# Second product of the MLP: block products and plain chunks of a tile in shared PSUM banks, plain parts between block parts, and the tail's loads and low parts in another order

## Chip, cores and metric

One of the eight cores of a Trainium2 chip runs the kernel. The metric is the device time of one execution in microseconds (us). The kernel before takes 654.17 us (median of 3 runs, 653.78 to 654.19). One further execution was profiled; all trace rows come from it.

## The reference

One transformer block on 512 tokens of width 1024: RMSNorm, a mixed attention, an output projection, and then the part that matters here:

```
h = rmsnorm(x, mlp_pre_g)
a, u = split(h @ w_gate_up, [2816])
a = causal_dwconv(a, conv_w, conv_b)
y = (gelu(a) * u) @ w_down            # 2816 -> 1024: the second product
x = x + rmsnorm(y, mlp_post_g)
e = p @ w_ple
x = x + e * sigmoid(x @ w_ple_gate)   # the gate product
```

Everything is float32. The kernel splits each operand of a product into a high part and a low part and makes three TensorE products (high x high, low x high, high x low).

## The kernel before, in words

Tiles are 128 rows (features) by 512 columns (tokens). `w_down` has 22 chunks of 128 inner features and 8 output tiles of 128 rows. Output tiles 0 and 1 are computed plainly in `mlp_down`. The other six are computed in `down_pairs` (L1620) as three pairs, c = 0, 1, 2, each with two tiles i = 0, 1.

**Plain chunks.** Ten of the 22 chunks are multiplied as usual: `rest(c, i, k)` (L1700) takes five of them for tile i, k = 0 or 1, 15 matmuls of 512 columns into a PSUM bank of the tile (tag "mm"). For the last pair, `last(h, i)` (L1820) does it by token halves h, 30 matmuls of 256 columns for a half tile, into banks of its own.

**Block products.** The other twelve chunks go in three groups g through a 2x2 block scheme with seven products in place of eight (two output tiles x two inner chunks x two token halves). `token` (L1635) makes the sums of the token side, `sums` (L1671) those of the weights, `products` (L1683) issues 42 matmuls of 256 columns per group: 18 with the weights as loaded (part 0) and 24 with their sums (part 1). They end in four banks per pair; `blocks` (L1709) adds those up, `aside` (L1728) copies the plain result out of its bank, `finish` (L1733) adds the two, `square` (L1737) adds the squares to the running sum `acc` for the norm.

**Order.** `down_pairs` writes its order by hand: every step is put at a time with `at(t, f)`, the list is sorted by time and issued, and each step is kept in program order on its engine. So the times are only an order per engine: ScalarE (ACT) makes the high parts (`high`, L1661) and squares, VectorE (DVE) the low parts (`low`, L1665), sums and adds, GpSimd (POOL) the additions to `acc` and some low parts, SyncE (SP) issues every load. A step waits for its operands and for a free slot of its tile's tag ("wr" 2 slots, "wh" 6, "p" 6, "u" 26); what stands behind it on the same engine waits too. TensorE (PE) runs: plain chunks of pair 0, block parts of 0, plain chunks of 1, block parts of 1, block parts of 2, plain chunks of 2.

**The tail.** While the last pair runs, SP loads the attention's result x1 (`fetch` 0 to 3), four tiles of `w_ple_gate` (`gate(n, 0)`, L1810), two more of them for the next stage (issued by `weight` in `ple_gate`, L248) and the tiles of e (`fetch` 4 to 7, "r_away"). `gate(n, 1)` and `gate(n, 2)` make their high and low parts; three of the four low parts are on POOL (L1815). `out` (L1834) finishes a half tile: DVE adds (L1837), ACT squares (L1839), DVE adds to `acc` (L1841). When token half 0 of all tiles is in `acc`, `rstd_col` (L282, four small matmuls, then DVE and POOL) and `rstd_row` (L295) make the norm's factor "r4a"; then `norm_half` (L1263) applies it tile by tile on DVE and ACT, and `gate_half` (L1608) multiplies the four gate tiles with the result, first for half 0, then for half 1. `ple_gate` does the other four gate tiles and the output.

Of the kernel before, what the change touches and what calls it, by code (L numbers as in the profile page):

```python
# [15 lines left out]
P = 128  # L16
T = 512
# [26 lines left out]

TTAG = ["p"] * 4 + ["kn", "tt", "pt"] + ["u"] * 5
# [134 lines left out]
class Block:  # L180
# [1439 lines left out]
    def down_pairs(self, acc, yo, first):  # L1620
# [61 lines left out]
        def products(c, g, part):  # L1682
            z = w[c, g]  # L1683
            if g == 0 and part == 0:
                st[c]["z"] = [self.ps(t) for t in (["t", "t", "mm", "mm"] if c == 2 else "ssso")]
            key = ("raw", "sum")[part]
            todo = (((0, 0, 2, 0), (1, 2, 0, 0), (2, 7, 1, 0)), ((1, 6, 2, 1), (2, 5, 3, 0), (0, 4, 1, 1), (3, 3, 0, 1)))[part]
            for i, b, bank, half in todo:
                o = st[c]["z"][bank][:, HALF[half]]
                for k in range(2):  # L1690
                    x = yt[2 * g + k][b]
                    m = slice(i * W + k * P, i * W + k * P + P)
                    keep(mm(o, z[key, 0][:, m], x[:, 0, :], start=g + k + half == 0, stop=False, skip_group_check=True))
                    mm(o, z[key, 1][:, m], x[:, 0, :], start=False, stop=False, skip_group_check=True)
                    mm(o, z[key, 0][:, m], x[:, 1, :], start=False, stop=g == 2 and k == 1, skip_group_check=True)

        def rest(c, i, k):
            z = st[c]
            if k == 0:
                z["x", i] = self.ps("mm")  # L1700
            self.ordered = True
            wt = w[c, "x", i, k]
            for n in range(5):
                self.mm3(z["x", i], (wt["raw", 0], wt["raw", 1]), n * P, plain[5 * k + n], k + n == 0, k + n == 5)
            self.ordered = False

        def blocks(c, n):
            z = st[c]["z"]
            if n == 0:  # L1709
                if c == 2:  # L1710
                    yo.append(self.u([P, 2, T]))
                st[c]["q"] = self.s([P, T])
                if c < 2:
                    st[c]["r"] = self.s([P, T])
# [3 lines left out]
            m, q, s = yo[c + 1], st[c]["q"], st[c]["s"]  # L1718
            if n == 1:
                keep(add(s, s, z[2][:, H:]))  # L1720
                keep(add(q[:, H:], s, z[1][:, H:]))
            if n == 2:
                keep(add(s, s, z[3][:, :H]))
                keep(add(m[:, 0, :], q, z[0]) if c == 2 else add(q, q, z[0]))
            if n == 3:
                keep(add(halves(m[:, 1, :] if c == 2 else st[c]["r"]), s[:, None, :].broadcast_to([P, 2, H]), halves(z[1])))

        def aside(c, i):  # L1728
            if i == 0:
                yo.append(self.u([P, 2, T]))  # L1730
            keep(act.activation(yo[c + 1][:, i, :], st[c]["x", i], AF.Copy))

        def finish(c, i):  # L1733
            m = yo[c + 1][:, i, :]
            keep(add(m, m, st[c]["r" if i else "q"]))

        def square(c, i):  # L1737
            m = yo[c + 1][:, i, :]
            sq = self.s([P, T])
            keep(act.activation(sq, m, AF.Square))  # L1740
            keep(nc.gpsimd.tensor_add(acc, acc, sq))
# [14 lines left out]
        for u in xs(0) + gs(0) + xs(1) + gs(1) + gs(2) + xs(2):  # L1756
# [49 lines left out]
        def gate(n, k):  # L1806
# [152 lines left out]
```

## Time and profile before

| | |
|---|---|
| median of 3 runs | 654.17 us |
| the profiled execution | 655.45 us |
| its span (first to last instruction) | 653.7 us |
| PE busy in the span | 637.4 us (98%) |
| DVE busy | 530.6 us (81%) |
| ACT busy | 384.2 us (59%) |
| POOL busy | 153.5 us (23%) |

Times in rows count from the start of the span. A row of the timeline gives start, duration, engine, line, operation, output<-inputs, shapes, count, and in brackets how long the engine had been idle and whom it waited for. Matmuls overlap: their distance from start to start, not the duration shown, is what PE needs for one. The second product of the MLP in pairs runs from about 506 to 602 us, the norm and the four gate tiles to 626.7, the rest to 653.7.

### The profile page before, as it was taken

To read this page: it belongs to the slowest core of one execution; us is meant where nothing else is said; L and a number is where in the kernel's file an instruction comes from. 1 tells how busy PE (TensorE), PEld (TensorE's weight loads), DVE (VectorE), ACT (ScalarE), POOL (GpSimd) and SP (SyncE) were. 2 spreads that over 40 slices of the span, in tenths; PEclk is the share of its full clock that TensorE was granted. 3 is DMA by queue.
4 is the path that set the end of the run, shared out by engine and by line. 5 is a ranking of instruction groups with operands and counts; after the bars stand their busy time and mean duration, and the time that the engine had idled before them with its cause. 6 is when DMAs were issued, how large, how long until landed. Compare 5 with 4: busy or idle time off the path is not lost.

```text
span 653.7 us, 10857 instructions
## 1 busy us (share of the span) xinstructions
PE 637.4 (98%) x3865; PEld 567.7 (87%) x3865; DVE 530.6 (81%) x1118; ACT 384.2 (59%) x745; POOL 153.5 (23%) x225
## 2 busy tenths in 40 slices
PE   8999999999999999999998999999999999997996
PEld 8988887888787888888888999999988888996985
DVE  7794878988897559588999999999769775885972
ACT  7554689879999456265555565655656544342351
POOL 1112598668484310032020000000000001033000
PEclk9999999999999999999999999999999999997999
DMA  8437622210236466222413332432131323583031
GB/s 300 164 106 218 193 71 72 58 50 26 74 109 216 142 220 231 65 64 98 157 39 127 129 122 73 130 97 98 57 90 60 117 81 109 163 312 141 2 130 65
DMA packets 27719, 78.05 MB, mean 119 GB/s; under 512 B 3473, under 2 KB 4753, under 8 KB 27665
## 3 DMA queue, kind: packets, MB, share of 16 engines
q1 hardware_dynamic: 27520, 77.28, 36.0%
q8 instruction: 30, 0.49, 0.3%
q14 instruction: 25, 0.20, 0.1%
q10 hardware_dynamic: 144, 0.08, 0.1%
HBM read 63.72 MB, written 6.29 MB: 107 GB/s over the span
## 4 chain that ended last, share of the span: by engine, by line
PE 70%; DVE 15%; ACT 7%; issue 4%; DMA 3%; POOL 1%; ACTq 0%; SPq 0%; DVEq 0%
PE strassen_pss L1436 3%; PE strassen_pss L1439 3%; PE strassen_pss L1440 3%; PE nsa_pst L803 2%; PE nsa_pso L818 2%; PE r_pss L1184 2%; PE r_psmm L1184 2%; PE strassen_pst L1440 2%; PE strassen_pst L1439 2%; PE strassen_pst L1436 2%; PE mlpdown_psmm L255 1%; PE mlpdown_psmm L258 1%; PE mlpdown_psmm L259 1%; PE strassen_psmm L1439 1%; PE strassen_psmm L1436 1%
## 5 line engine op out<-in xcount | busy, mean ns | idle before, releaser
L590 POOL TENSOR_SCALAR nsa_u<-nsa_u,nsa_nrc,gate 128x512 f32<-128x512 f32 (+3 forms) x64 | 38.5, 612 | 21.6 <-DVE nsa_nrc L710 10.2
L1436 PE MATMUL strassen_pss<-sums_u,strassen_u 128*128 128x256 f32 x144 | 40.5, 282 | 1.7 <-ACT strassen_s L1447 1.7
L1749 POOL TENSOR_TENSOR mlpdown_s<-mlpdown_s,mlpdown_s 128x512 f32<-128x512 f32 x1 | 1.3, 1291 | 171.8 <-ACT mlpdown_s L1747 171.8
L1439 PE MATMUL strassen_pss<-sums_u,strassen_u 128*128 128x256 f32 x144 | 40.5, 281 | 0.0
L1440 PE MATMUL strassen_pss<-sums_u,strassen_u 128*128 128x256 f32 x144 | 40.5, 281 | 0.0
L602 ACT ACTIVATE nsa_u<-nsa_u,nsa_nnm 128x512 f32<-128x512 f32 (+3 forms) x64 | 35.3, 553 | 3.6 <-DVE nsa_nnm L598 3.3
L811 DVE TENSOR_TENSOR nsa_u<-nsa_pst,nsa_u 128x512 fp32r<-128x512 f32 x40 | 27.0, 688 | 9.8 <-ACT nsa_u L807 9.6
L1398 DVE TENSOR_TENSOR strassen_u<-strassen_u,strassen_u 128x1024 fp32r<-128x1024 f32 x27 | 33.3, 1237 | 0.0
L1661 ACT ACTIVATE mlpdown_u<-mlpdown_u 128x1024 fp32r<-128x1024 f32 (+1 forms) x15 | 15.0, 1013 | 28.0 <-DVE mlpdown_u L1680 18.7
L1394 ACT ACTIVATE strassen_u<-strassen_u 128x1024 fp32r<-128x1024 f32 x27 | 28.4, 1052 | 1.2 <-DVE strassen_u L1410 1.1
L1436 PEld LDWEIGHTS strassen_pss<-sums_u,strassen_u 128*128 128x128 f32 x144 | 27.2, 189 | 1.9 <-ACT strassen_s L1447 1.9
L818 PE MATMUL nsa_pso<-nsa_u,vnatural_u 128*128 128x512 f32 x80 | 28.0, 422 | 0.0
L1439 PEld LDWEIGHTS strassen_pss<-sums_u,strassen_u 128*128 128x128 f32 x144 | 27.2, 189 | 0.1
L1440 PEld LDWEIGHTS strassen_pss<-sums_u,strassen_u 128*128 128x128 f32 x144 | 27.2, 189 | 0.0
L807 ACT ACTIVATE nsa_u<-nsa_pst 128x512 fp32r<-128x512 f32 x40 | 23.3, 594 | 4.7 <-PE nsa_pst L803 4.1
L1330 POOL TENSOR_TENSOR mlpup_s<-mlpup_s,r3b 128x512 f32<-128x512 f32 x7 | 14.0, 2004 | 47.8 <-ACT mlpup_s L1302 42.8
L598 DVE CUSTOM_DVE_ANT_0 nsa_u<-nsa_pss,biastables_u 128x320 f32<-128x320 f32 (+3 forms) x64 | 24.7, 413 | 0.6 <-PE nsa_pss L595 0.5
L1665 DVE TENSOR_TENSOR mlpdown_u<-mlpdown_wr,mlpdown_u 128x640 fp32r<-128x640 f32 (+1 forms) x19 | 18.1, 951 | 8.8 <-ACT mlpdown_u L1661 8.8
L803 PEld LDWEIGHTS nsa_pst<-ident,nsa_u 128*128 128x128 f32 x160 | 18.9, 140 | 6.9 <-DVE nsa_u L811 1.3
L1440 PE MATMUL strassen_pst<-sums_u,strassen_u 128*128 128x256 f32 x88 | 24.8, 281 | 0.0
L1439 PE MATMUL strassen_pst<-sums_u,strassen_u 128*128 128x256 f32 x88 | 24.8, 281 | 0.0
L1436 PE MATMUL strassen_pst<-sums_u,strassen_u 128*128 128x256 f32 x88 | 24.7, 281 | 0.0
(637 smaller groups left out, 2504.5 us busy)
## 6 DMA issues: line engine op xcount, KB each, us to landing
strassen_wr<-in_gu_dram SPq DMA_DIRECT2D x14, 512.0 KB, 4.6
strassen_u<-in_gu_dram SPq DMA_DIRECT2D x14, 512.0 KB, 3.8
mlpup_wr<-in_gu_dram SPq DMA_DIRECT2D x10, 512.0 KB, 3.3
mlpdown_wr<-in_dn_dram SPq DMA_DIRECT2D x9, 512.0 KB, 3.5
mlpdown_wr<-in_dnx_dram SPq DMA_DIRECT2D x10, 320.0 KB, 3.0
projq_wr<-in_win_dram SPq DMA_DIRECT2D x5, 512.0 KB, 3.5
loadx_u<-in_xT_dram SPq DMA_DIRECT2D x8, 256.0 KB, 4.9
compress_u<-projk_u SPq DMA_DIRECT2D x16, 128.0 KB, 2.3
```

What stands on the lines that cost most here:

```text
L590: self.tc.keep_in_program_order(self.nc.gpsimd.tensor_scalar(ap, ap, col, gate, op0=ALU.mult, op1=ALU.mult))
L598: self.tc.keep_in_program_order(self.nc.vector.tensor_tensor_reduce(dst, src, bias, op0=ALU.add, op1=ALU.min, scale=slope, scalar=first, a ...
L602: self.tc.keep_in_program_order(self.nc.scalar.activation(p, p, AF.Exp, bias=nm, scale=-1.0, accum_out=sm))
L803: keep(nc.tensor.transpose(pt[:, r * P : (r + 1) * P], src, self.ident))
L811: keep(nc.vector.tensor_sub(t[:, 1, :], u["pt", j], t[:, 0, :].bitcast(F32)))
L818: keep(nc.tensor.matmul(u["po"], v, u["t", j][:, part, :], start=start, stop=u["left"] == 0))
L1184: keep(mm(ps, z["w", f"up{i}"][k][:, c * P : c * P + P], x, start=c + part + k == 0, stop=c == KC - 1 and part == 1))
L1394: keep(act.activation(hi, src, AF.Copy))
L1398: keep(sub(lo, src, hi.bitcast(F32)))
L1436: r = mm(ps, hi[:, o], x[:, 0, :], start=fresh and p == 0, stop=False, skip_group_check=not fresh)
L1439: mm(ps, lo[:, o], x[:, 0, :], start=False, stop=False, skip_group_check=not fresh)
L1440: mm(ps, hi[:, o], x[:, 1, :], start=False, stop=p == Q - 1, skip_group_check=not fresh)
```

## The change

1. **Shared banks.** The block products that only one tile needs go into the bank in which that tile's plain chunks are accumulated ("C" for tile 0, "D" for tile 1); two more banks ("U", "V") hold the products that both tiles need. Each pair has four banks, with its own tags. For half 1 of the last pair the tiles have further banks ("C1", "D1"). `aside` and `finish` go; `blocks` is one ACT copy and four adds of 256 columns; `join` adds SBUF and PSUM in one step. PE's matmuls are the same ones.
2. **Order on PE.** The two plain parts of tile 1 of pair 1 move between the block parts of pairs 1 and 2. In the tail, `rstd_col` and `rstd_row` stand one and two chunks of 3 matmuls later.
3. **Squares.** The addition to `acc` (`total`) is a step of its own, on POOL for pair 0 and on DVE for pair 1.
4. **Token sums.** The subtractions for the last token tile (5) come 6.6 us earlier in the list (9.6 for 16.2); the rest of it keeps its place.
5. **Loads and low parts of the tail.** x1 is fetched ahead of the gate tiles, the four gate tiles come next, then the two tiles for the next stage (now in the list, on SP behind gate tile 3), then e. All four gate low parts are on DVE. Some tags change.

```diff
+BANK = [dict(C="mm", D="mm", U="t", V="t"), dict(C="s", D="o", U="s", V="s"), dict(U="mm", V="mm", C="t", D="t", C1="s", D1="o")]
...
+        def product(c, g, n):
             z = w[c, g]
+            key, i, b, name, half = (("raw", 0, 0, "U", 0), ("raw", 1, 2, "C", 0), ("raw", 2, 7, "D", 0), ("sum", 1, 6, "U", 1), ("sum", 2, 5, "V", 0),
+                                     ("sum", 0, 4, "V", 1), ("sum", 3, 3, "C", 1))[n]
+            if c == 2 and n == 6:
+                name, half = "C1", 0
...
         def blocks(c, n):
...
-                keep(act.activation(st[c]["s"], z[2][:, :H], AF.Copy))
-                keep(act.activation(st[c]["q"][:, :H], z[2][:, :H], AF.Copy))
...
+                keep(act.activation(st[c]["q"][:, :H], z["U"][:, :H], AF.Copy))
+            q, r, u = st[c]["q"], st[c]["r"], st[c]["s"]
             if n == 1:
+                keep(add(u, q[:, :H], z["U"][:, H:]))
+                keep(add(q[:, H:], u, z["V"][:, H:]))
             if n == 2:
+                keep(add(r[:, :H], u, z["V"][:, :H]))
+                keep(add(r[:, H:], r[:, :H], z["V"][:, H:]))
-        def aside(c, i):
...
-        def finish(c, i):
...
+        def join(c, i):
             if i == 0:
                 yo.append(self.u([P, 2, T]))
+            keep(add(yo[c + 1][:, i, :], st[c]["qr"[i]], st[c]["z"]["CD"[i]][0]))
         def square(c, i):
...
+        def total(c, i):
+            keep((vec if c else nc.gpsimd).tensor_add(acc, acc, st[c]["sq", i]))
...
-        for u in xs(0) + gs(0) + xs(1) + gs(1) + gs(2) + xs(2):
+        for u in xs(0) + gs(0) + xs(1)[:2] + gs(1) + xs(1)[2:] + gs(2) + xs(2):
...
-                at((-12.0, -9.0, -6.0, -3.0, 2.6, 16.2)[t] + 0.8 * n, lambda t=t, n=n: token(t, n))
+                at((-12.0, -9.0, -6.0, -3.0, 2.6, 16.2 if n else 9.6)[t] + 0.8 * n, lambda t=t, n=n: token(t, n))
...
-                high(u, tags=(("kn", "tt"), ("u", "u"), ("u", "u"), ("wh", "wh"))[n])
+                high(u, tags=(("kn", "tt"), ("pt", "pt"), ("u", "u"), ("tt", "u"))[n])
             if k == 2:
-                low(u, eng=nc.gpsimd if n else vec)
+                low(u)
...
+        for n in range(2):
+            at(z + 26.0 + 0.01 * n, lambda n=n: next_gate(n))
         for n in range(4):
-            at(z + (5.3, 6.8, 13.0, 14.4)[n], lambda n=n: fetch(n))
-            at(z + 22.0 + 1.5 * n, lambda n=n: fetch(4 + n))
+            at(z + 5.3 + n, lambda n=n: fetch(n))
+            at(z + 26.1 + 0.01 * n, lambda n=n: fetch(4 + n))
             for k in range(3):
-                at(z + (11.8 + (0, 4.2, 6.2)[k], 13.4 + (0, 4.4, 5.4)[k], 15.4 + (0, 4.9, 5.9)[k], 17.0 + (0, 9.2, 10.6)[k])[n], lambda n=n, k=k: gate(n, k))
+                at(z + (10.8 + (0, 6.0, 6.8)[k], 11.8 + (0, 7.0, 7.6)[k], 15.4 + (0, 4.8, 5.4)[k], 16.8 + (0, 5.0, 7.8)[k])[n], lambda n=n, k=k: gate(n, k))
...
-        at(x + 2 * h, lambda: last(1, 0, range(5)))
-        at(x + 2.5 * h, lambda: w4.update(c=self.rstd_col(acc[:, HALF[0]], "r4a")))
-        at(x + 2.5 * h + 0.1, lambda: last(1, 0, range(5, 10)))
-        at(x + 3 * h, lambda: w4.update(r=self.rstd_row(w4["c"], "r4a", copy=False)))
+        at(x + 2 * h, lambda: last(1, 0, 0))
+        at(x + 2 * h, lambda: last(1, 0, 1, range(1)))
+        at(x + 2 * h + 2.2, lambda: w4.update(c=self.rstd_col(acc[:, HALF[0]], "r4a")))
+        at(x + 2 * h + 2.3, lambda: last(1, 0, 1, range(1, 5)))
         at(x + 3 * h + 0.1, lambda: out(1, 0, 0))
-        at(x + 3 * h + 0.2, lambda: last(1, 1))
+        at(x + 3 * h, lambda: last(1, 1, 0, range(2)))
+        at(x + 3 * h + 0.72, lambda: w4.update(r=self.rstd_row(w4["c"], "r4a", copy=False)))
+        at(x + 3 * h + 0.73, lambda: last(1, 1, 0, range(2, 5)))
+        at(x + 3 * h + 0.74, lambda: last(1, 1, 1))
```

## Rows read from the trace of the kernel before

**Rows 1.** The page: busy us of each engine, share of the span, instructions.
```profile
PE 637.4 (98%) x3865; PEld 567.7 (87%) x3865; DVE 530.6 (81%) x1118; ACT 384.2 (59%) x745; POOL 153.5 (23%) x225
```

**Rows 2.** Waits of PE over the span: waiting line, whom it waited for, us in total, times, longest us (those of the second product and of the norm behind it).
```profile
PE mlpdown_pst L282 <- DVE mlpdown_s L1841: 4.0, 1, 4.0
PE mlpdown_pss L1694 <- DVE mlpdown_u L1665: 0.7, 1, 0.7
PE norm_pss L259 <- DVE norm_u L1280: 0.6, 1, 0.6
PE mlpdown_psmm L1694 <- DVE mlpdown_u L1665: 0.2, 1, 0.2
```

**Rows 3.** Timeline of PE: the first plain matmul of the tail, the matmuls on both sides of the wait, and the first one after the four gate tiles.
```profile
580.25 0.28 PE L255 MATMUL mlpdown_pss<-mlpup_u,mlpdown_u 128*128 128x256 f32 x1
...
588.97 0.28 PE L258 MATMUL mlpdown_pss<-mlpup_u,mlpdown_u 128*128 128x256 f32 x1
589.09 0.28 PE L259 MATMUL mlpdown_pss<-mlpup_u,mlpdown_u 128*128 128x256 f32 x1
593.41 0.98 PE L282 MATMUL mlpdown_pst<-ones,mlpdown_s 128*128 128x1 f32 x4 [4.04 <-DVE mlpdown_s L1841]
...
597.17 0.41 PE L258 MATMUL mlpdown_pss<-mlpup_u,mlpdown_u 128*128 128x256 f32 x1
597.39 0.41 PE L259 MATMUL mlpdown_pss<-mlpup_u,mlpdown_u 128*128 128x256 f32 x1
...
602.15 0.28 PE L258 MATMUL norm_pss<-norm_u,mlpdown_u 128*128 128x256 f32 x1
603.02 0.39 PE L259 MATMUL norm_pss<-norm_u,mlpdown_u 128*128 128x256 f32 x1 [0.59 <-DVE norm_u L1280]
...
626.68 0.40 PE L255 MATMUL plegate_pst<-norm_u,plegate_wh 128*128 128x512 f32 x1
```

**Rows 4.** Busy time in a stretch of 1 us behind the wait: stretch, its length, then PE, PEld, DVE, ACT and POOL busy (and instructions), PE's granted clock, DMA share, GB/s.
```profile
595.00:596.00 1.00, 1.00 (x7) 1.00 (x6) 0.00 (x0) 0.00 (x0) 0.38 (x1) 0.50 0.06 25
```

**Rows 5.** The chain of work that ended last, in order of time: start, us, what.
```profile
580.45 9.04 DMA mlpdown_u<-in_wpg_dram
...
590.90 2.37 DVE mlpdown_s L1841
```

**Rows 6.** Timeline of ACT in the tail: high parts of gate tiles 0 and 1, of gate tile 2, and the square of the second half tile.
```profile
581.82 2.00 ACT L1661 ACTIVATE mlpdown_u<-mlpdown_u 128x1024 fp32r<-128x1024 f32 x2
...
589.51 1.06 ACT L1661 ACTIVATE mlpdown_u<-mlpdown_u 128x1024 fp32r<-128x1024 f32 x1 [1.33 <-DMA mlpdown_u<-in_wpg_dram]
590.47 0.40 ACT L1839 ACTIVATE mlpdown_s<-mlpdown_u 128x256 f32<-128x256 f32 x1
```

**Rows 7.** Timeline of DVE in the tail: three low parts of the last pair's plain weights, the first add of `blocks`, the low part of gate tile 0, the addition of the second half tile's squares to `acc`, and the second tile's addition in the norm.
```profile
580.17 1.46 DVE L1665 TENSOR_TENSOR mlpdown_u<-mlpdown_wr,mlpdown_u 128x640 fp32r<-128x640 f32 x1 [0.65 <-ACT mlpdown_u L1661]
581.55 1.55 DVE L1665 TENSOR_TENSOR mlpdown_u<-mlpdown_u,mlpdown_u 128x640 fp32r<-128x640 f32 x2
583.02 0.41 DVE L1720 TENSOR_TENSOR mlpdown_s<-mlpdown_s,mlpdown_psmm 128x256 f32<-128x256 f32 x1
...
585.52 1.87 DVE L1665 TENSOR_TENSOR mlpdown_u<-mlpdown_u,mlpdown_u 128x1024 fp32r<-128x1024 f32 x1
...
590.90 2.36 DVE L1841 TENSOR_TENSOR mlpdown_s<-mlpdown_s,mlpdown_s 128x256 f32<-128x256 f32 x1 [1.87 <-ACT mlpdown_s L1839]
...
600.51 2.12 DVE L1275 TENSOR_TENSOR mlpdown_u<-mlpdown_u,mlpdown_u 128x256 f32<-128x256 f32 x1
```

**Rows 8.** Timeline of POOL in the tail: low parts of gate tiles 2 and 3.
```profile
590.64 2.34 POOL L1665 TENSOR_TENSOR mlpdown_u<-mlpdown_u,mlpdown_u 128x1024 fp32r<-128x1024 f32 x1 [4.33 <-ACT mlpdown_u L1661]
...
599.80 2.55 POOL L1665 TENSOR_TENSOR mlpdown_u<-mlpdown_u,mlpdown_u 128x1024 fp32r<-128x1024 f32 x1 [4.42 <-ACT mlpdown_u L1661]
```

**Rows 9.** Timeline of SP: issues of gate tile 1, of a tile for the next stage, of gate tile 3, and of the first two of e; then, for the four gate tiles, the time from issue to landing; then, from the page, the loads of the block weights: count, KB of one, median us to landing.
```profile
576.08 0.38 SPq L1810 DMA_DIRECT2D mlpdown_u<-in_wpg_dram  x1
579.54 0.33 SPq L248 DMA_DIRECT2D plegate_wr<-in_wpg_dram  x1
...
582.04 0.92 SPq L1810 DMA_DIRECT2D mlpdown_u<-in_wpg_dram  x1
583.01 1.53 SPq L1803 DMA_DIRECT2D mlpdown_u<-r_away  x2
...
DMA to landing us min/median/max: 4.4/7.7/10.0
...
mlpdown_wr<-in_dn_dram SPq DMA_DIRECT2D x9, 512.0 KB, 3.5
```

**Rows 10.** Busy time in stretches of 2 us: columns as in rows 4.
```profile
578.00:580.00 2.00, 2.00 (x19) 2.00 (x18) 1.51 (x2) 1.13 (x2) 0.58 (x2) 1.00 1.05 346
...
590.00:592.00 2.00, 0.00 (x0) 0.00 (x0) 1.10 (x1) 0.87 (x2) 1.36 (x1) 1.00 1.04 424
```

**Rows 11.** Timeline of DVE and PE in the block parts of pair 0: the low part of the sums of group 0, the first subtraction of token tile 5, the low part of the sums of group 1, and the matmul that waited for it.
```profile
520.58 1.22 DVE L1665 TENSOR_TENSOR mlpdown_u<-mlpdown_u,mlpdown_u 128x1024 fp32r<-128x1024 f32 x1 [1.18 <-ACT mlpdown_u L1661]
524.14 0.68 DVE L1639 TENSOR_TENSOR mlpdown_u<-strassen_u 128x512 f32<-128x512 f32 x1
526.56 1.22 DVE L1665 TENSOR_TENSOR mlpdown_u<-mlpdown_u,mlpdown_u 128x1024 fp32r<-128x1024 f32 x1
527.83 0.39 PE L1694 MATMUL mlpdown_pss<-mlpdown_u,mlpdown_u 128*128 128x256 f32 x1 [0.70 <-DVE mlpdown_u L1665]
```

More of the change, by code (lines that the diff above doesn't have):

```diff
@@ L1680, in sums @@
                 keep(sub(q[3], a[1], q[1]))
-        def products(c, g, part):
-            z = w[c, g]
[L1684 to L1701, printed above, removed]
-            wt = w[c, "x", i, k]
-            for n in range(5):
-                self.mm3(z["x", i], (wt["raw", 0], wt["raw", 1]), n * P, plain[5 * k + n], k + n == 0, k + n == 5)
-            self.ordered = False
+        def bank(c, n, tag, half=0):
+            st[c].setdefault("z", {})[n] = [self.ps(tag), half, True]
+        def at_bank(c, n, half):
+            z = st[c]["z"][n]
+            fresh, z[2] = z[2], False
+            return z[0][:, HALF[half]] if half < 2 else z[0], fresh
@@ new lines, in product @@
+        def product(c, g, n):
+            z = w[c, g]
+            key, i, b, name, half = (("raw", 0, 0, "U", 0), ("raw", 1, 2, "C", 0), ("raw", 2, 7, "D", 0), ("sum", 1, 6, "U", 1), ("sum", 2, 5, "V", 0),
+                                     ("sum", 0, 4, "V", 1), ("sum", 3, 3, "C", 1))[n]
+            if c == 2 and n == 6:
+                name, half = "C1", 0
+            if name not in st[c].get("z", {}):
+                bank(c, name, BANK[c][name])
+            for k in range(2):
+                o, fresh = at_bank(c, name, half)
+                x = yt[2 * g + k][b]
+                m = slice(i * W + k * P, i * W + k * P + P)
+                keep(mm(o, z[key, 0][:, m], x[:, 0, :], start=fresh, stop=False, skip_group_check=True))
+                mm(o, z[key, 1][:, m], x[:, 0, :], start=False, stop=False, skip_group_check=True)
+                mm(o, z[key, 0][:, m], x[:, 1, :], start=False, stop=g == 2 and k == 1, skip_group_check=True)
@@ new lines, in rest @@
+        def rest(c, i, k, h=2, js=range(5)):
+            wt = w[c, "x", i, k]
+            name = "CD"[i] + ("1" if h == 1 else "")
+            if name not in st[c].get("z", {}):
+                bank(c, name, BANK[c][name])
+            for n in js:
+                o, fresh = at_bank(c, name, 0 if h == 1 else h)
+                y = plain[5 * k + n][:, :, HALF[h]] if h < 2 else plain[5 * k + n]
+                m = slice(n * P, n * P + P)
+                keep(mm(o, wt["raw", 0][:, m], y[:, 0, :], start=fresh, stop=False, skip_group_check=True))
+                mm(o, wt["raw", 1][:, m], y[:, 0, :], start=False, stop=False, skip_group_check=True)
+                mm(o, wt["raw", 0][:, m], y[:, 1, :], start=False, stop=k + n == 5, skip_group_check=True)
@@ L1791, in down_pairs @@
                 at(b + 1.25, lambda v=v: low(v, "sum"))
-            at(t, lambda u=u: products(*u))
+            for n in ((0, 1, 2), (3, 4, 5, 6))[part]:
+                at(t, lambda v=v, n=n: product(*v, n))
             if g == 2 and part == 1:
-                for i in range(4):
+                for i in range(3):
                     at(t + G * 4 / 7 + 0.2 + 0.4 * i, lambda c=c, i=i: blocks(c, i))
@@ L1844, in down_pairs @@
         w4 = {}
-        at(x, lambda: last(0, 0))
+        for i in range(2):
+            for k in range(2):
+                at(x + h * i + h / 2 * k, lambda i=i, k=k: last(0, i, k))
         at(x + h + 0.1, lambda: out(0, 0, 0))
-        at(x + h, lambda: last(0, 1))
         at(x + h + 0.9, lambda: out(0, 0, 1))
@@ L1870, in ple_gate @@
         nc, io = self.nc, self.io
-        ahead = {c: self.weight(io["wpg"][c], keep=True) for c in (NB, NB + 1)}
+        ahead = {NB + i: self.weight(r, early=True, keep=True) for i, r in enumerate(self.raws)}
         for c in range(KC):
```

50 lines of the change are left out of this document (18 added, 32 removed).

## The prediction

> **What bounds the kernel now.** I read the page first: PE is busy for 637.4 of 653.7 us, DVE for 530.6 [rows 1]. So only PE's waits, PE's clock and the ends are to be had; work taken from DVE or ACT counts only where PE waits for it. The table of PE's waits gives the places [rows 2]: one of 4.0 us at L282, and 0.7, 0.6 and 0.2 us in the second product and the norm behind it. The timeline shows what the longest costs [rows 3]. PE's matmuls of 256 columns start every 0.12 us (588.97, 589.09), then none until 593.41: 4.32 - 0.12 = 4.2 us. Afterwards they start every 0.21 to 0.22 us (597.17, 597.39), for the granted clock is 0.50 [rows 4], the lower of PE's two levels, 1.2 for 2.4 GHz. From 593.41 to the first matmul of the norm, 0.12 before 602.15, are 8.6 us; at 0.12 each, its 45 matmuls need 5.4, and the six small ones about 0.55, so the clock costs 8.6 - 5.95 = 2.65. The wait of 0.59 behind it costs 0.87 - 0.12 = 0.75. Together **7.6 us**. A cross-check: from 580.25 to 626.68 are 46.4 us [rows 3], for 120 half-wide plain matmuls and 192 of the gate tiles at 0.12 (37.4) and twice 0.55 for the norm's small ones, 38.5: 7.9 us more than the work.
>
> What ended the 4.2 us is read backwards. The last link is DVE's addition of the squares to `acc`, 590.90, 2.36 us long [rows 5, 7]; the third such addition and its like of 256 columns take about 0.42, but beside it POOL made the low part of gate tile 2 from 590.64 to 592.98 [rows 8]. Before it stands ACT's square at 590.47, queued behind the high part of gate tile 2 at 589.51, which waited for its load [rows 6], issued 580.45 and 9.04 us under way [rows 5]. So a weight that is needed in the next stage held up, in two engines' order, a sum on which PE waited. The 0.6 us wait later has the same cause: the norm's second addition took 2.12 us beside POOL's low part of gate tile 3 [rows 7, 8].
>
> **The change, part by part.** Count times from the first plain matmul of the tail (580.25 before) as T.
>
> *Gate low parts on DVE.* Nothing of the tail is left on POOL but the norm's small power, so the 2.36 and the 2.12 us go back to about 0.42: 3.6 us off both chains. DVE pays with two more low parts of 1024 columns, 1.22 us [rows 11], before the r4a chain, and one behind it.
>
> *Shared banks.* In the last pair `blocks` loses its two adds of 512 columns and one ACT copy, and has four of 256; from 583.02 to 585.52 it took 2.5 us [rows 7]; four dependent ones of 0.41 take about 1.7. PE's matmuls are the same. For pairs 0 and 1 four ACT copies and four adds of 512 per two pairs go, against joins; no PE wait hangs on them, cost nothing.
>
> *The chain to r4a.* DVE's order after T: the low parts of the plain weights, which ended at 583.02, T + 2.8, one of them taking 1.46 where its like take 0.78 [rows 7]: without that, T + 2.1. Then blocks 1.7, low parts 0, 1 and 2 at 1.15 each from start to start, add and `acc` of the first half tile 0.75: T + 8.0. Then the second half tile's add 0.4, ACT's square 0.5 with the handover, `acc` 0.45, handover to PE 0.1: T + 9.45. PE gets to the small matmuls after 60 + 18 matmuls, T + 9.36 (the change puts them one chunk later than T + 9.0). So PE waits about 0.1; with DVE as late as before (T + 2.8) 0.8. I take 0.2. The second step, `rstd_row`, has 18 matmuls or 2.2 us of cover for DVE's and POOL's steps of two columns: hidden. Should DVE take low part 3 first (1.22), it just fits.
>
> *Loads.* This holds if gate tiles 0 to 3 have landed when ACT comes to them: T + 1.3, 2.4, 5.6 and 6.7. SP now issues them right after x1 and the last plain weights, ahead of two tiles for the next stage and four of e, all of 0.5 MB. What blocks SP before them is the last "wr" slot, free when the sums of the last group are done, some 5.5 us before T, and a "u" slot each, released in steps from T - 9 to T. So gate tiles 1 to 3 can be issued between T - 5 and T. At 346 GB/s, as moved at 578 to 580 [rows 10], the three tiles and what is left of gate 0 need 6 us: landed by T + 1 to T + 6. Bounds by rows: 4.4 to 10.0 us from issue to landing [rows 9]; issued at T - 4, even 10.0 us suffices for tiles 2 and 3; issued at T it doesn't. I take no wait. What is late next: nothing until e, which the last stage reads 40 us later.
>
> Here a rule is weighed against a row. Gate tile 2 took 9.04 us, in which at 346 to 424 GB/s [rows 10] 6 to 7 tiles moved, though only five at most (gate 1 of 576.08, two x1 tiles, the one of 579.54 [rows 9] and itself) were issued up to then: it shared the engines with those issued behind. The Trainium skill, "DMA: Bandwidth & Descriptors", section "Queues, rings and completion order", has descriptors of one issuing engine consumed in ring order. The trace differs: by that rule, tile 2 would have landed by 587 or so, not 589.5, and after the change a gate tile would never wait for what stands behind it: the rival below would fall, with the sum as it is.
>
> *The norm behind.* Once `rstd_row` is on time, DVE begins the norm some 2.9 us before PE ends its plain matmuls, and its first tile takes 2.1 us. No wait: 0.75 us gone.
>
> *Block parts.* The subtractions of token tile 5 at 524.14 took DVE 1.6 us, right before the low part for which PE waited 0.7 us [rows 11]. They move ahead of the low part at 520.58, where DVE idled 1.18 us [rows 11]; that low part ends 0.4 us later, and PE, which came to it as it ended, waits about 0.2. The next one still stands behind the rest of token tile 5 and its ACT step, and its own chain begins later: the 0.7 us stay, with 0.2 more. So **+0.4 us**, between -0.9 (that wait goes) and +1.5 (the whole 1.6 us come on top). Pair 1's block parts now follow 6.8 us of plain matmuls instead of 13.6; the load of its first weights waits for a "wr" slot that the plain weights hold. That load (3.5 us, the median of its like [rows 9]) and then high, low, sums, joins, high and low, worked out one behind the other, end about 0.7 us before PE needs them. So 0, and a load longer by 2 us costs 1.3. The two plain parts put behind pair 1 give DVE 6.8 us to catch up: the 0.2 us wait of the last pair goes.
>
> *Sum.* 7.6 - 0.2 (rest at r4a) + 0.2 - 0.4 = 7.2 us less: 653.7 to 646.5 in the span. The profiled execution took 655.45, the median 654.17; less 7.2 that is **647.0 us**, a forecast with bounds 645.3 (all 8.9 us of waits and clock go) and 648.7 (0.8 at r4a, 1.5 in the block parts).
>
> **Rivals.**
>
> *A gate tile lands late* (faster, but by less). If the "u" slots bind until T and the tiles share with e, 9 to 10 us from issue put tile 3 at T + 9 or 10. ACT's high part stands before the square again, so PE waits 2 to 3 us and perhaps finds the lower clock. For it: the 9.04 us row. Against: two of its competitors, x1 tiles, are done before. 649 to 651.5.
>
> *The block parts starve* (as before). Pair 1's first weights land 2 to 3 us later than the row says, squares now stand in ACT's order before the high part of the sums, and each group hands its lateness on, since DVE's 4.75 us per group leave only 0.3 in PE's 5.04. Needs some 7 us in all to undo the tail: 653 to 655.
>
> *Slower.* The place is ACT's order in the tail: the high part of gate tile 3 stands ahead of the square on which r4a waits; before the change it stood behind r4a. Its landing decides: by T + 6.7 nothing is lost; from high part to PE are 2.0 us, so each us later is a us of PE's wait. PE came to it at 593.41, T + 13.2 before; that is reached with a landing at T + 11. Tile 3 was issued at 582.04; with that issue and the longest landing seen, 10.0, it comes at T + 11.8 [rows 9], so PE goes on at T + 13.9, 0.7 us later than before, at the lower clock; with 1.5 in the block parts and the norm's 0.75 off, 655.6. Against: its issue is freed of the tile of the next stage that stood before it.
>
> *It does not do what it says.* PE could keep the order of before, if the waits of shared banks forced it; the order is kept by hand, so I give this nothing of its own.
>
> **Chances.** Forecast 0.58, late gate tile 0.20, starved block parts 0.10 (half of it still ahead by over 0.2%), slower 0.12. A measurement of this kernel tells about 0.2%, 1.3 us, from no change. Faster 0.83, same 0.06, slower 0.11. The range takes the forecast's bounds and most of the late tile: 645.2 to 651.0; outside lie the rest of the late tile, half of the starved case and the slower one.
>
> **What would show it.** Right: no wait of PE at L282 over 0.5 us, granted clock 1.0 throughout the tail, DVE's additions to `acc` at 0.42, the four gate high parts on ACT without a wait for a load, 38.5 to 39 us from the first half-wide plain matmul to the first one of the next stage. Wrong: a wait at L282 with ACT's high part of gate tile 2 or 3 behind a load; or waits at the low parts of sums in pairs 0 and 1 that add up to over 2 us.

## The result and the profile after

The kernel after took 649.55 us (median of 8 runs, 649.12 to 652.44), the kernel before beside it 653.94 (8 runs, 652.85 to 654.47): ratio 0.9943, 95% interval 0.9928 to 0.9958. So it is faster, by 0.57%, and the time lies in the range; the gain is 4.4 us of the 7.2 forecast. The profiled execution took 649.33, with a span of 647.5.

The page first, the row that answers to [rows 1]:

```profile
PE 635.2 (98%) x3865; PEld 565.1 (87%) x3865; DVE 527.7 (81%) x1120; ACT 380.3 (59%) x738; POOL 143.8 (22%) x220
```

PE has lost 2.2 us of busy time without losing an instruction; matmuls at half clock count as busy for longer [rows 3, 4]. The waits of PE in the second product, which answer to [rows 2] (of the norm none is left):

```profile
PE mlpdown_pst L1704 <- DVE mlpdown_u L1666: 0.6, 1, 0.6
PE mlpdown_pst L283 <- DVE mlpdown_s L1850: 0.5, 1, 0.5
...
PE mlpdown_pss L1704 <- DVE mlpdown_u L1666: 0.2, 1, 0.2
```

The timeline of PE at the places of [rows 3]: the tail's first plain matmul, both sides of the wait, the norm's first matmul, the next stage.

```profile
581.02 0.28 PE L1716 MATMUL mlpdown_pst<-mlpup_u,mlpdown_u 128*128 128x256 f32 x1
...
590.22 0.28 PE L1718 MATMUL mlpdown_pss<-mlpup_u,mlpdown_u 128*128 128x256 f32 x1
591.03 0.61 PE L283 MATMUL mlpdown_pst<-ones,mlpdown_s 128*128 128x1 f32 x4 [0.54 <-DVE mlpdown_s L1850]
...
596.80 0.28 PE L256 MATMUL norm_pss<-norm_u,mlpdown_u 128*128 128x256 f32 x1
...
620.49 0.40 PE L256 MATMUL plegate_pst<-norm_u,plegate_wh 128*128 128x512 f32 x1
```

Between 590.22 and 591.03 are 0.81 us, 0.69 more than a matmul's 0.12, where 4.2 were lost before. From 581.02 to 620.49 are 39.47 us, against 46.43. The granted clock in the same stretch as [rows 4], then ACT's high parts and squares [rows 6], DVE [rows 7] and POOL [rows 8] in the tail:

```profile
595.00:596.00 1.00, 1.00 (x11) 1.00 (x10) 0.93 (x3) 0.42 (x1) 0.00 (x0) 1.00 0.00 0
```

```profile
580.85 0.74 ACT L1662 ACTIVATE mlpdown_u<-mlpdown_wr 128x640 fp32r<-128x640 f32 x1 [3.68 <-DMA mlpdown_wr<-in_dnx_dram]
...
583.01 2.00 ACT L1662 ACTIVATE mlpdown_u<-mlpdown_u 128x1024 fp32r<-128x1024 f32 x2
...
587.38 1.99 ACT L1662 ACTIVATE mlpdown_u<-mlpdown_u 128x1024 fp32r<-128x1024 f32 x2
590.11 0.42 ACT L1848 ACTIVATE mlpdown_s<-mlpdown_u 128x256 f32<-128x256 f32 x1 [0.73 <-DVE mlpdown_u L1846]
```

```profile
582.36 1.55 DVE L1666 TENSOR_TENSOR mlpdown_u<-mlpdown_u,mlpdown_u 128x640 fp32r<-128x640 f32 x2
583.83 0.42 DVE L1728 TENSOR_TENSOR mlpdown_s<-mlpdown_s,mlpdown_psmm 128x256 f32<-128x256 f32 x1
...
585.41 1.22 DVE L1666 TENSOR_TENSOR mlpdown_u<-mlpdown_u,mlpdown_u 128x1024 fp32r<-128x1024 f32 x1
586.54 0.41 DVE L1846 TENSOR_TENSOR mlpdown_u<-mlpdown_s,mlpdown_pst 128x256 f32<-128x256 f32 x1
...
588.46 1.23 DVE L1666 TENSOR_TENSOR mlpdown_u<-mlpdown_u,mlpdown_u 128x1024 fp32r<-128x1024 f32 x1
589.60 0.41 DVE L1846 TENSOR_TENSOR mlpdown_u<-mlpdown_s,mlpdown_pst 128x256 f32<-128x256 f32 x1
590.55 0.43 DVE L1850 TENSOR_TENSOR mlpdown_s<-mlpdown_s,mlpdown_s 128x256 f32<-128x256 f32 x1 [0.54 <-ACT mlpdown_s L1848]
...
591.76 1.21 DVE L1666 TENSOR_TENSOR mlpdown_u<-mlpdown_u,mlpdown_u 128x1024 fp32r<-128x1024 f32 x1
```

```profile
591.92 1.62 POOL L289 TENSOR_TENSOR r4ac<-mlpdown_rv,mhalf 128x2 f32<-128x2 f32 x1 [45.53 <-DVE mlpdown_rv L287]
```

The reader is to see that no high part of a gate tile waits for a load, that the addition to `acc` is back at 0.43, and that ACT instead waited 3.68 us for the load of plain weights (0,1), so that DVE's `blocks` began at 583.83, 2.8 us behind the first plain matmul, as late as before. ACT's high parts of gate tiles 2 and 3 (587.38) and DVE's low part of tile 2 (588.46) still stand ahead of the second half tile's square (590.11) and add (589.60); they only come earlier. Last the block parts [rows 11], DVE, POOL and PE: the wait of pair 0 is still there, and pair 1 has a new one.

```profile
526.55 0.69 DVE L1649 TENSOR_TENSOR mlpdown_u<-mlpdown_u,mlpdown_u 128x512 fp32r<-128x512 f32 x1 [1.73 <-ACT mlpdown_u L1648]
527.16 1.22 DVE L1666 TENSOR_TENSOR mlpdown_u<-mlpdown_u,mlpdown_u 128x1024 fp32r<-128x1024 f32 x1
...
545.16 2.04 DVE L1666 TENSOR_TENSOR mlpdown_u<-mlpdown_wr,mlpdown_u 128x768 fp32r<-128x768 f32 x1
```

```profile
544.40 1.99 POOL L1744 TENSOR_TENSOR mlpdown_s<-mlpdown_s,mlpdown_s 128x512 f32<-128x512 f32 x1 [0.24 <-ACT mlpdown_s L1741]
```

```profile
528.43 0.39 PE L1704 MATMUL mlpdown_pst<-mlpdown_u,mlpdown_u 128*128 128x256 f32 x1 [0.62 <-DVE mlpdown_u L1666]
...
551.14 0.39 PE L1704 MATMUL mlpdown_pss<-mlpdown_u,mlpdown_u 128*128 128x256 f32 x1 [0.23 <-DVE mlpdown_u L1666]
```

### The profile page after: what moved, and what is told of

The parts are those of the page before. It is cut to its first block, busy times and chain, and to the rows that moved or that the text cites. A ratio compares the mean times of both kernels' runs of the same rounds, so it can differ in the third digit from the quotient of the medians.

```text
span 647.5 us, 10830 instructions
## 1 busy us (share of the span) xinstructions
PE 635.2 (98%) x3865; PEld 565.1 (87%) x3865; DVE 527.7 (81%) x1120; ACT 380.3 (59%) x738; POOL 143.8 (22%) x220
## 4 chain that ended last, share of the span: by engine, by line
PE 64%; DVE 19%; ACT 7%; issue 4%; DMA 4%; POOL 1%; ACTq 0%; DVEq 0%; SPq 0%
DVE mlpdown_u L1666 3%; PE strassen_pss L1440 2%; PE strassen_pss L1441 2%; PE strassen_pss L1437 2%; PE nsa_pst L804 2%; PE nsa_pso L819 2%; PE r_pss L1185 2%; PE r_psmm L1185 2%; PE strassen_pst L1440 2%; PE strassen_pst L1437 2%; PE strassen_pst L1441 2%; PE strassen_psmm L1437 1%; PE strassen_psmm L1440 1%; PE strassen_psmm L1441 1%; ACT mlpdown_u L1662 1%
```

## The experiments

Two questions were open: where the 2.8 us between forecast and result went, and which part of the change made the gain. The table holds all kernels: median, ratio with its interval to the kernel before as it ran beside this one (in one batch of runs); then, from the profile, A = from the first plain matmul of pair 0 to that of the tail, B = from there to the next stage, and the time that PE lost at r4a's small matmuls.

| kernel | median us | ratio | A us | B us | at r4a us |
|---|---|---|---|---|---|
| before, as profiled | 654.17 | | 74.14 | 46.43 | 4.20 |
| before again | 654.03 | 1.0007 (0.9996 to 1.0018) | 74.02 | 45.66 | 3.44 |
| after | 649.55 | 0.9943 (0.9928 to 0.9958) | 74.40 | 39.47 | 0.69 |
| after again | 648.97 | 0.9935 (0.9922 to 0.9947) | 74.37 | 39.38 | 0.61 |
| after, low parts on POOL | 653.03 | 0.9994 (0.9983 to 1.0005) | 74.00 | 43.05 | 2.79 |
| after, old loads | 649.15 | 0.9936 (0.9923 to 0.9949) | 74.32 | 40.06 | 1.30 |
| after, old order | 648.39 | 0.9929 (0.9915 to 0.9943) | 74.86 | 38.65 | 0 |
| before, low parts on DVE | 653.67 | 1.0006 (0.9997 to 1.0015) | 74.09 | 45.13 | 3.31 |
| before, high part 2 later | 651.80 | 0.9973 (0.9962 to 0.9985) | 74.18 | 42.40 | 1.42 |
| before, both | 650.74 | 0.9960 (0.9946 to 0.9974) | 74.02 | 41.76 | 1.41 |
| after, three moves | 647.16 | 0.9908 (0.9894 to 0.9921) | 73.42 | 38.89 | 0.12 |
| old order, moves | 647.33 | 0.9909 (0.9895 to 0.9923) | 73.64 | 38.66 | 0 |
| three moves, token split | 647.17 | 0.9903 (0.9889 to 0.9917) | 72.78 | 38.96 | 0.19 |

**Before again.** No edit.

> The kernel before, unchanged, profiled once more. Open is why the medians lie 4.4 us apart and the two profiled executions 6.1. Theory A (the sum took its main term from one long execution): before's wait at the small matmuls of r4a and the half clock behind it change from execution to execution with the landing of gate tile 2; the other executions lie at 652.9 to 654.5, this profile shows a wait at L282 of 2 to 3.5 us instead of 4.0, and the mean clocks of the runs spread from 0.995 to 1.0. Rival B (the 7.6 us are in each execution of before, and the kernel after loses 2 to 3 us elsewhere in its timed runs): wait 4.0 us and half clock again, mean clock 0.995 in all runs.

The wait was 3.3 us, 3.44 lost, and the times ran from 652.39 to 655.18. The mean clocks of before's 35 runs in this batch spread from 0.993 to 0.999; the four at 0.999 took 652.1 to 652.45, all others 652.27 to 655.18. So the first half of A holds: before varies. The mean clock alone does not give the time, though (at 0.995 the runs lie from 652.27 to 655.18), and the profiled execution of 655.45, on which the sum stood, is longer than each of these 35 and of the eight beside the kernel after. The wait of 2.0 to 3.5 us was expected because of the load; ACT, POOL and DVE of this execution show what else there is:

```profile
588.45 1.04 ACT L1661 ACTIVATE mlpdown_u<-mlpdown_u 128x1024 fp32r<-128x1024 f32 x1
589.49 0.42 ACT L1839 ACTIVATE mlpdown_s<-mlpdown_u 128x256 f32<-128x256 f32 x1
```

```profile
584.27 2.40 POOL L1665 TENSOR_TENSOR mlpdown_u<-mlpdown_u,mlpdown_u 128x1024 fp32r<-128x1024 f32 x1 [3.63 <-ACT mlpdown_u L1661]
589.56 2.34 POOL L1665 TENSOR_TENSOR mlpdown_u<-mlpdown_u,mlpdown_u 128x1024 fp32r<-128x1024 f32 x1 [2.89 <-ACT mlpdown_u L1661]
```

```profile
585.22 2.54 DVE L1665 TENSOR_TENSOR mlpdown_u<-mlpdown_u,mlpdown_u 128x1024 fp32r<-128x1024 f32 x1
...
589.94 2.25 DVE L1841 TENSOR_TENSOR mlpdown_s<-mlpdown_s,mlpdown_s 128x256 f32<-128x256 f32 x1 [0.54 <-ACT mlpdown_s L1839]
```

Here the high part of tile 2 waits for no load, and PE still loses 3.44 us. So the second half of A, that the landing of tile 2 makes the wait, falls; the late load of [rows 5, 6] was worth some 0.8 us (4.20 - 3.44). The next suspect was POOL's work beside DVE's.

**Low parts back on POOL.** `low(u, eng=nc.gpsimd if n else vec)` in `gate` of the kernel after.

> After, with the low parts of gate tiles 1 to 3 back on POOL, nothing else. Theory (the two engines slow each other): POOL's low part of tile 2 stands beside the additions of the second half tile on DVE, they take 1.4 to 2.4 us instead of 0.42, r4a comes 1 to 1.5 us later than PE instead of 0.6, and POOL's power of r4a waits behind the low part of tile 3 or is beside it: 1 to 2.5 us slower than after (650.5 to 652). Rival (DVE's own queue was the limit): with 2.4 us less on DVE ahead of r4a the wait at L283 goes, 0.7 us faster than after (648.8).

Slower than after by 3.5 us (649.55, of another batch), nearly all of the gain; the rival falls. Low part 0 took 3.15 us, the addition to `acc` 1.42, PE's wait was 2.63, and behind it the granted clock was 0.50:

```profile
584.62 3.15 DVE L1666 TENSOR_TENSOR mlpdown_u<-mlpdown_u,mlpdown_u 128x1024 fp32r<-128x1024 f32 x1
...
590.84 1.42 DVE L1850 TENSOR_TENSOR mlpdown_s<-mlpdown_s,mlpdown_s 128x256 f32<-128x256 f32 x1 [1.44 <-ACT mlpdown_s L1848]
```

```profile
589.64 2.34 POOL L1666 TENSOR_TENSOR mlpdown_u<-mlpdown_u,mlpdown_u 128x1024 fp32r<-128x1024 f32 x1 [2.95 <-ACT mlpdown_u L1662]
```

```profile
594.00:596.00 2.00, 2.00 (x11) 2.00 (x11) 0.42 (x1) 0.39 (x1) 2.00 (x1) 0.50 0.00 0
```

The theory named the mechanism and left out the clock, so its 1 to 2.5 us were too few.

**Old loads.** The kernel after with before's places for x1, the gate tiles and e, and the tiles of the next stage loaded in their own stage; the high and low parts keep their places of the kernel after:

```diff
...
-            at(z + 5.3 + n, lambda n=n: fetch(n))
-            at(z + 26.1 + 0.01 * n, lambda n=n: fetch(4 + n))
+            at(z + (5.3, 6.8, 13.0, 14.4)[n], lambda n=n: fetch(n))
+            at(z + 22.0 + 1.5 * n, lambda n=n: fetch(4 + n))
...
```

> After, with the loads of the tail at the places of before (x1 in two pairs, gate tiles 0 to 3 at 11.8, 13.4, 15.4, 17.0, e behind, the two tiles of the next stage not ahead of e but in their own stage); high and low parts as after. Theory (the late load is the cause of before's wait): gate tiles 2 and 3 land 589 to 591, the high part of tile 3 stands ahead of the second square on ACT, r4a is 3 to 4 us late, PE's clock falls to 0.50 behind it: 3 to 7 us slower than after (652.5 to 656.5). Rival (the low parts on DVE and the order did it, loads are hidden): within 0.7 us of after.

Going by the time, my theory fell: 649.15, as after. Three high parts waited for loads, that of tile 1 for 1.12 us and these two in front of the square:

```profile
587.31 1.06 ACT L1662 ACTIVATE mlpdown_u<-mlpdown_u 128x1024 fp32r<-128x1024 f32 x1 [1.71 <-DMA mlpdown_u<-in_wpg_dram]
588.57 1.06 ACT L1662 ACTIVATE mlpdown_u<-mlpdown_u 128x1024 fp32r<-128x1024 f32 x1 [0.19 <-DMA mlpdown_u<-in_wpg_dram]
590.06 0.42 ACT L1845 ACTIVATE mlpdown_s<-mlpdown_u 128x256 f32<-128x256 f32 x1 [0.43 <-DVE mlpdown_u L1843]
```

DVE's low part of tile 2 then waits for that high part, and the second half tile's add stands behind it:

```profile
588.40 1.23 DVE L1666 TENSOR_TENSOR mlpdown_u<-mlpdown_u,mlpdown_u 128x1024 fp32r<-128x1024 f32 x1 [1.85 <-ACT mlpdown_u L1662]
589.55 0.42 DVE L1843 TENSOR_TENSOR mlpdown_u<-mlpdown_s,mlpdown_pst 128x256 f32<-128x256 f32 x1
```

So here a late load does end the wait at r4a, but PE loses only 1.30 us there. DVE's earlier work was done in good time: plain weights (0,1) did not hold up ACT, and `blocks` began at 581.96, 1.6 us behind the tail's first plain matmul instead of 2.8. The new places of the loads are worth 0.6 us of B in the profile and nothing that the times show.

**Old order.** The kernel after with `xs(1) + gs(1)` and token tile 5 wholly at 16.2.

> After, with PE's order of units as before (all four plain parts of pair 1 ahead of its block parts) and token tile 5 at its old time; shared banks and the tail as after. The sum gave the new order and the earlier subtractions +0.2 us net. Theory: 0.2 to 0.3 us faster than after, and the wait before pair 1's last block part (0.40) goes while that at the last pair (0.2 before) comes back. Rival (the plain parts between give DVE room it needs): 1 to 2 us slower than after.

Not slower, and not to be told from after by its interval. The last pair lost 1.02 us at a low part (0.2 were expected), and r4a nothing. So the block parts neither starve without the new order and the earlier subtractions nor gain by them.

**After again.** No edit.

> The kernel after, unchanged, beside the others of this job. Theory (only the kernel before varies by the half clock behind its wait): its runs carry mean clocks of 0.998 to 1.0, its wait at the small matmuls of r4a is again 0.5 to 0.8 us, and its profile again takes 39.3 to 39.7 us from the tail's first plain matmul to the next stage; median 649 to 650. Rival: the wait varies here too, and the stage takes over 40.5 us in this profile.

As the theory has it; clocks 0.998 to 1.0, times 648.8 to 649.3.

**Low parts on DVE alone.** In the kernel before, `low(u)` for `low(u, eng=...)`.

> Before, with one part of the change alone: the low parts of gate tiles 1 to 3 on DVE; loads, order, banks as before. Theory (POOL beside DVE is the larger part of before's wait): the low part of tile 0 takes 1.2 us instead of 1.9 to 2.5, the additions to acc 0.4 instead of 2.3, the wait at L282 shrinks from 3.4 to 4.2 to 1 to 2 us, the clock stays at 1.0 or nearly: 650 to 651.5, some 3 us faster than before. Rival (the late load of gate tile 2 was the cause, as the prediction read it): DVE now stands behind the low part of tile 2, which waits for the load, so the wait stays over 3 us and the time within 1 us of before.

The theory fell: 653.67, no gain. The rival came true in place and number, but the low part of tile 2 waits for ACT's order more than for the load: the load landed at 588.76, and the high part, which stands behind the first square, began at 588.79 without a wait shown. The addition to `acc` is at 0.42; what stands in front of it is new. DVE's timeline:

```profile
585.55 2.35 DVE L1665 TENSOR_TENSOR mlpdown_u<-mlpdown_u,mlpdown_u 128x1024 fp32r<-128x1024 f32 x2
587.82 0.41 DVE L1837 TENSOR_TENSOR mlpdown_u<-mlpdown_u,mlpdown_pss 128x256 f32<-128x256 f32 x1
588.79 0.43 DVE L1841 TENSOR_TENSOR mlpdown_s<-mlpdown_s,mlpdown_s 128x256 f32<-128x256 f32 x1 [0.55 <-ACT mlpdown_s L1839]
589.88 1.23 DVE L1665 TENSOR_TENSOR mlpdown_u<-mlpdown_u,mlpdown_u 128x1024 fp32r<-128x1024 f32 x1 [0.67 <-ACT mlpdown_u L1661]
591.02 0.41 DVE L1837 TENSOR_TENSOR mlpdown_u<-mlpdown_u,mlpdown_pss 128x256 f32<-128x256 f32 x1
591.98 0.42 DVE L1841 TENSOR_TENSOR mlpdown_s<-mlpdown_s,mlpdown_s 128x256 f32<-128x256 f32 x1 [0.54 <-ACT mlpdown_s L1839]
```

The low part of tile 2 stands ahead of the second half tile's add and waits for ACT's high part, which ran right behind the first square. That gave a third theory, order (what stands ahead of the second half tile's sum in ACT's and DVE's order sets the wait), and two runs for it.

**Both, and high part 2 later.** In the kernel before, ACT's high part and the low part of tile 2 go behind the second square, first with the low parts on DVE ("both"), then on POOL as they were. The entry of tile 2 within its line of the list:

```diff
...
-15.4 + (0, 4.9, 5.9)[k]
+15.4 + (0, 7.4, 9.6)[k]
...
```

> Before, with the low parts of gate tiles 1 to 3 on DVE (as e5) and, beyond e5, the high part of tile 2 on ACT behind the second half tile's square and its low part on DVE behind it; loads, banks and units as before. Theory (what stands ahead of the second half tile's sum in ACT's and DVE's order sets the wait, whichever engine it runs on and whether or not its load is late): add at 588.2, square, acc at 589.7, PE waits 1.0 to 1.6 us instead of 3.3, PE's clock stays at 1.0: 39.5 to 41 us from the tail's first plain matmul to the next stage instead of 45.1; 649 to 650. Rival (it took the earlier DVE work and the shared banks of the change as well): the wait stays above 2.5 us, 652 or more.

> Before, with gate tile 2's high part alone moved behind the second square (its low part on POOL follows it); all low parts stay on the engines of before. Theory: the addition to acc of 2.3 us is back at 0.42, the wait at L282 shrinks from 3.4 to 4.2 to 1.5 to 2.2 us (low part 0 on DVE still 1.9 to 2.5 us beside POOL's low part 1), the clock may fall in some runs: 650.5 to 652. Rival (the engine is what matters): over 652.5.

With the low parts on POOL, moving one tile's high part, and the low part that follows it, takes 1.8 us off the time (651.80, where 650.5 to 652 were expected): the square runs at once, the addition meets no work of POOL's, and the granted clock stays at 1.00. ACT, DVE and the granted clock of that kernel:

```profile
589.98 0.42 ACT L1839 ACTIVATE mlpdown_s<-mlpdown_u 128x256 f32<-128x256 f32 x1 [0.95 <-DVE mlpdown_u L1837]
590.30 1.04 ACT L1661 ACTIVATE mlpdown_u<-mlpdown_u 128x1024 fp32r<-128x1024 f32 x1
```

```profile
590.43 0.43 DVE L1841 TENSOR_TENSOR mlpdown_s<-mlpdown_s,mlpdown_s 128x256 f32<-128x256 f32 x1 [0.54 <-ACT mlpdown_s L1839]
```

```profile
594.00:596.00 2.00, 2.00 (x19) 2.00 (x18) 1.50 (x3) 1.37 (x2) 1.47 (x2) 1.00 0.16 64
```

Part of it comes back at the norm's first matmul, where PE loses 1.53 us; with the low parts on DVE it is 0.64. The order theory holds for the wait (1.42 and 1.41 us), not in full for the time: the kernel with both took 650.74, above the 649 to 650 expected, and B is 2.3 us above that of after. Of these, 0.7 are lost at r4a and 1.04 at the norm's first two tiles (0.64 and 0.40), where after loses nothing; there DVE's low part of tile 3 (594.91, 1.23 us) stands ahead of the norm's first operation (596.05). Which parts of the change remove that (the shared banks with their shorter `blocks`, the places of adds and low parts, r4a's places) was not tried part by part; no run takes the shared banks alone out or in.

**Three moves.** The kernel after with its three waits attacked (token tile 5 split behind the low part; the plain weights (1,1) ahead of the late (0,1); the additions of pair 0's squares on DVE, where it idles):

```diff
...
-16.2 if n else 9.6)[t]
+16.3 if n else 9.6)[t]
...
-(0, 1): 2.2, (1, 0): 4.8, (1, 1): 3.2}
+(0, 1): 3.2, (1, 0): 4.8, (1, 1): 2.2}
...
-at(done + 3.0, lambda c=c, i=i: total(c, i))
+at(done + (3.0 if c else 20.4 - 0.65 * i), lambda c=c, i=i: total(c, i))
...
-keep((vec if c else nc.gpsimd).tensor_add(acc, acc, st[c]["sq", i]))
+keep(vec.tensor_add(acc, acc, st[c]["sq", i]))
...
```

> After, with three moves aimed at its three waits: the split of token tile 5 one step later, behind DVE's low part of the sums (wait 0.78); the additions of pair 0's squares from POOL to DVE, at a place where DVE idles (wait 0.40, behind a low part of 2.04 us beside POOL); the high and low part of plain weights (1,1) ahead of those of (0,1), which land late (wait 0.69 at r4a). Theory: the three waits go, 113.9 us from the first plain matmul of pair 0 to the next stage become 112.0 to 112.4, 647.6 to 648.2. Rival (DVE is full there, so each move shifts the wait to the next low part): 113.5 or more, 649 to 650.

All three waits went (0.12 us are still lost at r4a); 0.60 us came at the next low part of pair 0. A + B is 112.31, as expected, the time of 647.16 a little below; after had 648.97 in the same batch, and the two intervals do not overlap. This version beats both kernels.

**Old order with moves.** The old order, token tile 5 and plain weights as in the three moves, pair 1's additions at `when[2, 1, 1] + 0.5` and `when[2, 2, 0] + 2.0`.

> The order-old kernel (e3: PE's units as before, the rest as after) with token tile 5 subtracted early and split behind the low part, the plain weights (1,1) ahead of (0,1), and the two additions of pair 1's squares, which stood ahead of the low parts for which PE waited 1.02 us, put where DVE idles. Theory: e3's waits of 0.79 and 1.02 go, at most 0.3 comes at r4a: 113.5 us of the stage become 111.7 to 112.1, 646.6 to 647.4, the fastest. Rival: without the 1.02 us PE comes to r4a early and waits there for as much: 113 us, 648 to 648.5.

The waits of 0.79 and 1.02 went, 0.60 and 0.25 came: A + B 112.30 us where 111.7 to 112.1 were expected, the time of 647.33 as expected, and as fast as the three moves.

**Token split.** Three moves, and of token tile 5 the second half first, the first half 3.65 behind its place.

> e6 with the remaining wait of 0.60 us (before the last block part of pair 0) attacked: of token tile 5 only the half that the raw products need is split ahead of them, the other half behind the sums of the last group. Theory: the wait goes, 112.3 us of the stage become 111.7 to 111.9, 646.5 to 646.9. Rival (DVE has no room there, it waits one low part later): 112.2 or more, as e6.

The wait went, and A + B fell from 112.31 to 111.74 us, as expected; at r4a 0.19 were lost for 0.12. The time of 647.17 is that of the three moves and above the 646.5 to 646.9 expected: half a microsecond is not to be told here.

## Why the prediction was right in direction and 2.5 us low

- **What failed: carrying the sum over to the median.** Against the execution that it was made from, the sum was nearly right. B was to lose 7.6 - 0.2 = 7.4 us and lost 6.96; A was to grow by 0.2 and grew by 0.26. The two spans lie 6.2 apart, since the profiled execution of after also entered the stage 0.5 us later (506.62 against 506.11). But the 7.2 were taken from the median of 654.17, and 655.45 less 7.2 is 648.2. So of the 2.8 us by which the gain fell short, 1.5 are the distance from the profiled execution to the median beside the kernel after (653.94), 0.5 the stage, 0.5 its later start, and the rest lies between after's profile and its median. With more runs before's median is 653.2 to 654.0, and the profiled execution lies 1.4 to 2.3 above it. That this distance is of the wait and half clock which the change takes away is argued, not shown: of the 1.1 us between the two profiled executions of before, 0.77 lie in B, and how many us of wait each timed run had was not seen. The mean clocks of before spread and those of after do not, so the clock varies in before; yet one run of after took 652.44 us at a mean clock of 1.0, and no profile shows why.
- **Wait and clock (7.6 us).** Right as rows. The cause was ranked wrongly: the text read the chain back to the 9.04 us load. With the load in time before loses 3.44 us all the same, and in the kernel after with the old loads, where a late load does end the wait, PE loses only 1.30. What counts in the kernel before is the work of the next stage ahead of r4a's sum: a high part on ACT, and beside or ahead of the sum a low part, on either engine.
- **Low parts on DVE.** The 2.36 and 2.12 us fell to 0.43 as said. That this part by itself gives nothing before (653.67) was not foreseen. The rows show what else the change does: counted from the tail's first plain matmul, the first half tile's add runs at 5.5 us in after (586.54) and at 7.5 in before with the low parts on DVE (587.82). Of the 2.0 us, 0.9 come from the shorter `blocks` (low part 0 begins at 4.4 for 5.3), and 1.1 are the low part of tile 1, which stood ahead of the add and now stands behind it. ACT's first square, and the high part of tile 2 behind it, come about as much earlier. No run tries these two alone.
- **Rest at r4a.** 0.69 instead of 0.2: the case "as late as before, 0.8" that the text named and did not take. Plain weights (0,1), issued at 575.45 with four loads of 320 to 512 KB ahead of them still under way, landed after 5.3 us; in the kernel before they took 3.0.
- **Loads.** No wait of a high part: right; gate tiles 1 to 3 were issued at T - 5.2 to T - 4.2 and landed at T + 1.0 to T + 3.6. With the old loads it was worth 0.6 us at r4a. A slip without effect: 10.0 us from T - 4 would not have sufficed for tile 2, which was needed at T + 5.6. The rule of the Trainium skill, "DMA: Bandwidth & Descriptors", section "Queues, rings and completion order", that the text set against the 9.04 us row, was not decided: in the kernel before as in the kernel after, every load that SP issued from 570 to 585 landed in its order of issue (before, those of 579.54, 579.92 and 580.45 at 585.38, 586.67 and 589.49), which ring order would give as well. Why 2.8 us lie between the last two stays open.
- **Block parts.** +0.4 - 0.2 forecast, +0.26 measured; that the two are close is luck. The wait of pair 0 was to grow by 0.2 and shrank (0.86 us lost before, 0.78 after), the one of 0.2 at the low part before it did not come, and the last pair's went (0.36 lost before). Not foreseen: 0.40 us in pair 1, where POOL's addition of pair 0's squares stands beside DVE's low part (2.04 us). These come to nothing; the 0.26 are spread over matmuls without a wait.
- **Rivals.** No gate tile landed late. The slower case, high part 3 behind a late load, did not come even with the old loads, where that tile's high part (588.57, 1.06 us) ended 0.43 us before the square began; what a late load held there was DVE's low part of tile 2. The blocks did not starve, in either order.

## What to carry to other kernels

When one wait dominates and the clock falls behind it, compare the profiled execution with the spread of the timed runs before taking a sum from the median: the same stall may be what makes the profiled one long. When a wait's chain ends in a load, ask what would end it if the load were early, and look at what else stands ahead in each engine's order; moving work of the next stage behind the sum that is waited for was worth 1.8 us with two numbers changed. An operation taken off one engine helps only if the same sum does not come to wait behind it on the other: the low parts on DVE gave nothing in the kernel before, and in the kernel after, where they come early enough, nearly all of the gain hangs on them.

## What was not expected of the hardware

- DVE's operations with two SBUF inputs beside POOL's are not stretched in proportion; in these rows they end a fixed time behind it. The addition of 256 columns, 0.42 us alone, ended 0.28 to 0.29 us behind POOL's low part in three executions (593.26 and 592.98 before [rows 7, 8]; 592.19 and 591.90 before again; 592.26 and 591.98 with the low parts on POOL), however much of it had lain beside POOL: 2.36, 2.25 and 1.42 us. Adds that take one input from PSUM kept their time beside POOL: in the kernel before those of `blocks` at 583.99, 584.33 and 584.92 took 0.42, 0.68 and 0.68 us beside POOL's low part of 583.90 to 586.32, as they do with POOL idle (0.42, 0.68 and 0.68 with both). It goes both ways: POOL's power of two columns, 0.71 us in the kernel before, took 1.62 beside DVE's low part of tile 3 in the kernel after, and 1.63 in the kernel with both.

```profile
594.67 0.71 POOL L288 TENSOR_TENSOR r4ac<-mlpdown_rv,mhalf 128x2 f32<-128x2 f32 x1 [1.69 <-DVE mlpdown_rv L286]
```

The Trainium skill, "SBUF — State Buffer", section "SBUF: two separate sides", says that the port pair shared by the two is locked for a whole instruction by the one that starts first, a POOL operation or a DVE operation with two SBUF inputs, and the other blocks. These rows agree.

- The granted clock behind the wait was 0.50, the lower of the two levels, where PE had idled 2.6 to 4.0 us (before, before again, low parts on POOL, low parts on DVE), and 1.00 where it had idled 1.4 (at the norm with high part 2 later) or less. So such a wait cost more than itself: from before again to high part 2 later PE lost 2.0 us less at r4a, and B fell by 3.3, although 1.45 us more were lost at the norm's first tiles (1.92 for 0.47).
